# A hybrid attention decoder layer on one core: the out-projection weights' transfers moved from SyncE's queue to GpSimd's, their low parts to a buffer of their own

## Chip, cores, metric

The kernel runs on one core of one Trainium2 chip. The metric is the device time of one execution in microseconds (us); a kernel's time is the median of its runs. Engines are named as in the profile: PE (TensorE, matmuls), PEld (TensorE's weight loads), DVE (VectorE), ACT (ScalarE), POOL (GpSimd), SP (SyncE, which here only issues DMAs). Each engine works through its own queue in order; an instruction that waits holds up everything behind it on that engine.

## The reference, cut to what matters

One layer, sequence 1024, width 1024, float32:

```python
h = rms_norm(x, pre_g)
z = h @ w_in                       # 1024 x 7184: q, k, v, gate for 8 attention heads,
                                   # q, k, v, gate for 4 gated heads, 16 columns for the decay
oa = diff_attention(qa, ka, va, lam)   # softmax(q1 k1) - lam * softmax(q2 k2), causal
oa = rms_norm(oa, subln_g) * (1 - lam_init) * silu(ga)
ob = gla_chunked(qb, kb, vb, log_a)    # gated linear attention
ob = rms_norm(ob, gla_g) * silu(gb)
y = concat([oa, ob]) @ w_out       # 2048 x 1024
out = x + rms_norm(y, post_g)
```

Matmuls keep float32 accuracy by splitting each operand in a high part (rounded to TensorE's fp32r format) and a low part (the rest), and by summing three products: high by high, low by high, high by low.

## The kernel before, in words

**Stages.** First (to about 640 us) the in-projection; in its last two thirds the gated heads run between its steps. Then attention of the eight heads, with the out-projection of finished parts woven in, and a short end. Matmuls are issued through `mm` (line 117), which pins them: the order of PE's instructions is the program's. The other engines' orders are made by the framework's scheduler, which takes the instructions as their inputs and buffers come free in its own simulated time.

**The in-projection.** `pairs` lists 28 blocks of 256 columns of `w_in`. Each is computed by a Strassen-like scheme in seven products, numbered 1, 2, 5, 6, 4, 7, 3; `order` lists all (pair, product). A step (`step`, called by `go`) is one entry: 12 matmuls of 512 columns, or 24 of 256 columns in each of two pairs that run side by side ("wide" pairs, for values). `load_raw` (line 194) fetches a pair's raw weights from SP in two halves (`w_raw`, four buffers). `make_weights` subtracts blocks on DVE (line 296), rounds to the high part on ACT (315) and takes the low part on DVE (316), up to four steps ahead into a ring of five buffers. After product 1, 6 and 7 ACT copies a bank (`s`, 427); DVE adds (440); results go by way of the buffers `c` and `st`, four of each, to DRAM from SP (367, 377 and others).

**The out-projection's weights.** `w_out` (2048 x 1024) is split in high and low parts once, during the in-projection, and the parts go back to DRAM (`wod`), from where `weights` (909) loads them for the out-projection. `wo_step(n)`, called by `go` after each step of pairs 6 and up (n is the product's number), does this for one block of 128 x 512 floats (256 KB) at a time; there are 32 blocks:

- at n = 1 or 6 it takes the block that is open: ACT rounds it to `wo_hi` (584; a buffer of the ring `c`), DVE writes the low part over the raw block (586), and SP stores both (588);
- at n = 2 or 4 it opens the next one: SP loads 256 KB of `w_out` into `wo_raw` (592).

`wo_raw` has a single buffer. As the low part lies in it, the next load can't start before the low part's store has landed.

**The gated heads.** `gla`, a generator of which `go` runs one piece after each step from (12, 5) on, works through 4 heads in 2 halves each. `gla_loads` (745) fetches queries, keys, values (`kq`, `gv`) and the decayed queries `gqd` (754), the latter into a buffer with the tag `q1`, which has room for 1024 floats a partition and of which `gqd` takes 512. POOL's only work in this part is the causal select on the scores of a half, `gan` (775), which the matmuls `gpo` read some steps later. After the in-projection `load_qk` puts the first head's queries into `q1`.

Of the kernel before, what the change touches and what calls it, by code (L numbers as in the profile page):

```python
# [8 lines left out]
F32 = mybir.dt.float32  # L9
F32R = mybir.dt.float32r  # L10
# [4 lines left out]
P = 128  # L15
# [16 lines left out]
def hymba_kernel(  # L32
# [21 lines left out]
    act, dve, pool, pe, sp = nc.scalar, nc.vector, nc.gpsimd, nc.tensor, nc.sync  # L54

    def fp(t):
        return t.bitcast(F32)

    def cols(half):
        return slice(half * 512, half * 512 + 512)  # L60
# [38 lines left out]
    wod = [tc.dram_tile([2, P, D], F32, name=f"wo{e}_d") for e in range(2 * D // P)]  # L99
# [53 lines left out]
    kp = ctx.enter_context(tc.tile_pool(name="kp", bufs=1))  # L153
# [6 lines left out]
    def t_c(name, dt=F32):  # L160
        return t2k("c", 4, name, dt)
# [413 lines left out]


    wo_todo = [(e % 16, dh) for e in range(8, 24) for dh in range(2)]
    wo_open = []

    def wo_step(n):  # L580
        if n in (1, 6) and wo_open:
            e, dh, raw = wo_open.pop()
            hi = t_c("wo_hi", F32R)
            act.copy(hi, raw)
            lo = raw.bitcast(F32R)
            dve.tensor_tensor(lo, raw, fp(hi), ALU.subtract)
            for t, src in enumerate((hi, lo)):
                sp.dma_start(wod[e][t][:, cols(dh)], fp(src))
        if n in (2, 4) and wo_todo:
            e, dh = wo_todo.pop(0)  # L590
            raw = ap.tile([P, 512], F32, tag="t4", name="wo_raw", bufs=1)
            sp.dma_start(raw, w_out[0, e * P : (e + 1) * P, cols(dh)])
            wo_open.append((e, dh, raw))

    def go(n):
        for _ in range(n):
            i = made[0]
            if i == len(order):
                return
            made[0] = i + 1  # L600
            for a in range(4):
                prepare(i + a)
            step(i)
            if order[i][0] > EARLY and not (wide(order[i][0]) and order[i][0] % 2):
                wo_step(order[i][1])
            if fill and next(fill[0], 0) == 0:
                fill.pop(0)
# [135 lines left out]
    def gla_loads(g, half):  # L743

        if g < GLA_HEADS and (g, half) not in loaded:
            cs = cols(half)
            kq = kp.tile([P, 2, 512], F32, tag="q0", name="kq")
            v = kp.tile([P, 2, 4, P], F32, tag="k0", name="gv")
            qd = kp.tile([P, 512], F32, tag="q1", name="gqd")
            sp.dma_start(kq[:, 0], gq_d[g][2, :, cs])  # L750
            sp.dma_start(kq[:, 1], gq_d[g][0, :, cs])
            for t in range(2):
                sp.dma_start(v[:, t], gv_d[g][t, :, half * 4 : half * 4 + 4, :])
            sp.dma_start(qd, gq_d[g][1, :, cs])
            loaded[g, half] = kq, v, qd
        return loaded.get((g, half))

    def gla(g):

        u = None  # L760
        for half in range(2):
            cs = cols(half)
            kq, v, qd = gla_loads(g, half)
            gates = kp.tile([P, 2, 512], F32, tag="ks1", name="gg")
            yield
# [43 lines left out]
            for m in range(2):  # L809
# [13 lines left out]
                free.append(ib)  # L823
            yield
            gla_loads(*((g, 1) if half == 0 else (g + 1, 0)))

            sqs = kp.tile([P, 2, 512], F32, tag="k1", name="sqs")
# [697 lines left out]
```

## Time and profile before

| | us |
|---|---|
| median of 3 runs | 981.83 |
| all runs | 981.83, 982.66, 979.48 |
| the profiled execution | 982.58 |
| its span, first to last instruction | 980.8 |
| PE busy in the span | 957.4 (98%) |
| DVE busy | 735.6 (75%) |
| ACT busy | 600.6 (61%) |
| POOL busy | 138.9 (14%) |

The 1.8 us between the span and the profiled execution's time lie outside the first and last instruction. "Busy" for PE runs to modelled ends of pipelined matmuls. A wait in the lists below reads: engine, what it was about to do, line, then "<-" and what ended the wait; total us, times, longest.

### The profile page before, as it was taken

Reading aid. Unit: us, or ns where it says so; the run is one execution under the profiler, and the core shown is the slowest. Engines: PE = TensorE matmul, PEld = TensorE weight load, DVE = VectorE, ACT = ScalarE, POOL = GpSimd, SP = SyncE. Lnnn points to the kernel's source line nnn. Section 1 sums busy time; section 2 is a strip of 40 time slices with the busy share of each in tenths; the row PEclk is TensorE's granted clock in tenths of the full one; section 3 lists DMA queues with packets and bytes.
Section 4 is the critical chain, followed back from the end, with each engine's and each line's share of the span. In section 5 each row is a group of like instructions: output and inputs, shape, how many; then the busy total and the mean of one; then the engine's idle time right before and its main releaser. Section 6 shows DMA issues by size and latency. Waiting matters only on the chain.

```text
span 980.8 us, 15654 instructions
## 1 busy us (share of the span) xinstructions
PE 957.4 (98%) x5282; PEld 828.7 (84%) x5282; DVE 735.6 (75%) x1452; ACT 600.6 (61%) x1164; POOL 138.9 (14%) x158
## 2 busy tenths in 40 slices
PE   5999999999999999999999999999999999999997
PEld 5998988888889998899887888878888888888785
DVE  6887597798866677586785876487888888898554
ACT  8742455487357455445465775365777687887773
POOL 4300000000000010000000101121322222443322
PEclk9999999999999999999999999999999999999999
DMA  9442456656674868887887766997656769995777
GB/s 348 146 112 90 137 137 206 229 174 234 239 245 160 265 202 275 246 265 253 284 256 241 258 207 186 413 290 247 217 167 222 243 198 353 345 283 112 151 208 146
DMA packets 152593, 220.45 MB, mean 225 GB/s; under 512 B 17104, under 2 KB 83664, under 8 KB 152416
## 3 DMA queue, kind: packets, MB, share of 16 engines
q1 hardware_dynamic: 146176, 203.71, 64.2%
q0 software_dynamic: 6336, 15.73, 7.1%
q8 instruction: 42, 0.69, 0.3%
q14 instruction: 39, 0.32, 0.1%
HBM read 133.93 MB, written 88.60 MB: 227 GB/s over the span
## 4 chain that ended last, share of the span: by engine, by line
PE 83%; DVE 5%; DMA 5%; ACT 3%; issue 2%; SPq 1%; POOL 0%; DVEq 0%; ACTq 0%; POOLq 0%
PE x L117 20%; PE ypart L117 13%; PE y L117 13%; PE z L117 13%; PE sc L117 7%; PE po L117 5%; PE yps L117 4%; PE wtr L120 3%; PE gpo L117 1%; DMA w_raw<-in_w_in_dram 1%; DMA wo_raw<-in_w_out_dram 1%; DVE w L316 1%; DMA wo_d<-wo_raw 1%; PE gkl_ps L117 1%; DMA x<-in_x_dram 1%
## 5 line engine op out<-in xcount | busy, mean ns | idle before, releaser
L315 ACT CAST w<-w_raw 128x512 fp32r<-128x512 f32 (+1 forms) x164 | 112.2, 688 | 91.3 <-PE y L117 43.2
L316 DVE TENSOR_TENSOR w<-w_raw,w 128x512 fp32r<-128x512 f32 (+1 forms) x164 | 126.3, 773 | 51.6 <-ACT w L315 44.7
L1048 ACT ACTIVATE p<-p,stt 128x896 f32<-128x896 f32 (+7 forms) x128 | 99.3, 777 | 36.8 <-DVE stt L1038 34.0
L427 ACT COPY s<-x 128x512 f32<-128x512 f32 x84 | 49.1, 585 | 87.6 <-PE x L117 87.2
L296 DVE TENSOR_TENSOR w_raw<-w_raw 128x512 f32<-128x512 f32 (+1 forms) x96 | 75.8, 789 | 16.1 <-DMA w_raw<-in_w_in_dram 14.7
L1038 DVE CUSTOM_DVE_ANT_0 p<-sc,maskt 128x512 f32<-128x512 f32 (+3 forms) x128 | 74.2, 584 | 14.6 <-PE sc L117 13.5
L775 POOL TENSOR_SCALAR_AFFINE_SELECT gan<-gan 128x512 f32<-128x512 f32 x8 | 12.7, 1588 | 493.7 <-ACT gan L774 493.7
L117 PE MATMUL x<-s_hi,w 128*128 128x512 f32 x320 | 79.9, 392 | 1.9 <-ACT s L427 1.9
L117 PE MATMUL y<-h_hi,w 128*128 128x512 f32 x320 | 79.9, 392 | 0.0
L117 PE MATMUL ypart<-wo_hi,m_hi 128*128 128x512 f32 x192 | 79.5, 414 | 0.1
L117 PE MATMUL z<-s_hi,w 128*128 128x512 f32 x320 | 79.6, 391 | 0.0
L1054 POOL TENSOR_SCALAR p<-p,stt,lam 128x1024 f32<-128x1024 f32 (+3 forms) x64 | 56.1, 876 | 147.0 <-DVE stt L1053 144.6
L117 PE MATMUL ypart<-wo_hi,m_lo 128*128 128x512 f32 x192 | 75.5, 393 | 0.0
L117 PE MATMUL ypart<-wo_lo,m_hi 128*128 128x512 f32 x192 | 75.4, 393 | 0.0
L117 PEld LDWEIGHTS x<-s_hi,w 128*128 128x128 f32 x320 | 59.8, 188 | 14.5 <-ACT s L427 2.3
L117 PE MATMUL sc<-k,q 128*128 128x512 f32 (+1 forms) x192 | 69.1, 363 | 1.2 <-DVE stt L1038 1.2
L117 PEld LDWEIGHTS y<-h_hi,w 128*128 128x128 f32 x320 | 59.8, 188 | 12.3
L117 PEld LDWEIGHTS z<-s_hi,w 128*128 128x128 f32 x320 | 59.5, 188 | 12.0
L117 PE MATMUL sc<-ks,q 128*128 128x512 f32 (+1 forms) x192 | 66.1, 347 | 0.0
L1096 ACT CAST wt_hi<-wtr 128x512 fp32r<-128x512 f32 (+1 forms) x80 | 42.7, 534 | 24.8 <-PE wtr L120 24.0
L1097 DVE TENSOR_TENSOR wt_lo<-wtr,wt_hi 128x512 fp32r<-128x512 f32 (+1 forms) x80 | 50.6, 632 | 8.8 <-ACT wt_hi L1096 8.0
L1057 DVE SCALAR_TENSOR_TENSOR p<-p,stt,p 128x1024 f32<-128x1024 f32 (+3 forms) x64 | 52.1, 813 | 4.1 <-POOL p L1054 3.8
(226 smaller groups left out, 2245.0 us busy)
## 6 DMA issues: line engine op xcount, KB each, us to landing
w_raw<-in_w_in_dram SPq DMA_DIRECT2D x56, 512.0 KB, 4.6
wo_raw<-in_w_out_dram SPq DMA_DIRECT2D x32, 256.0 KB, 3.0
wo_d<-wo_hi SPq DMA_DIRECT2D x32, 256.0 KB, 2.7
wo_d<-wo_raw SPq DMA_DIRECT2D x32, 256.0 KB, 2.7
q<-q_d SPq DMA_DIRECT2D x32, 256.0 KB, 4.9
k<-k_d SPq DMA_DIRECT2D x32, 256.0 KB, 5.6
ks<-k_d SPq DMA_DIRECT2D x64, 128.0 KB, 5.8
v<-v_d SPq DMA_DIRECT2D x16, 512.0 KB, 7.6
```

Of the source, the lines that this page charges most:

```text
L117: tc.keep_in_program_order(pe.matmul(*a, **k))
L120: tc.keep_in_program_order(pe.transpose(dst, src, ident))
L296: dve.tensor_tensor(dst, a, b, ALU.subtract)
L315: act.copy(w[0], src)
L316: dve.tensor_tensor(w[1], src, fp(w[0]), ALU.subtract)
L427: act.copy(b[k], ps)
L1038: ins = dve.tensor_tensor_reduce(p[:, a:e], sc[:, : e - a], maskt[:, NZ + P - (e - a) :] if last else maskt[:, : e - a], 1.0, 3e38 if i == ...
L1048: act.activation(p[:, :n], p[:, :n], AF.Exp, bias=st[:, m : m + 1], scale=-1.0, accum_out=st[:, 2 + m : 3 + m],)
L1054: pool.tensor_scalar(p1[:, :n], p1[:, :n], st[:, 5:6], lam, ALU.mult, ALU.mult)
L1057: dve.scalar_tensor_tensor(p0[:, :n], p0[:, :n], st[:, 4:5], p1[:, :n], ALU.mult, ALU.subtract)
L1096: act.copy(hi[:, :n], pt[:, :n])
L1097: dve.tensor_tensor(lo[:, :n], pt[:, :n], fp(hi[:, :n]), ALU.subtract)
```

## The change

```diff
-    wo_open = []
+    wo_open, spare = [], []
 
     def wo_step(n):
         if n in (1, 6) and wo_open:
             e, dh, raw = wo_open.pop()
             hi = t_c("wo_hi", F32R)
             act.copy(hi, raw)
-            lo = raw.bitcast(F32R)
+            lo = (spare[0][:, 1] if spare else raw).bitcast(F32R)
             dve.tensor_tensor(lo, raw, fp(hi), ALU.subtract)
             for t, src in enumerate((hi, lo)):
-                sp.dma_start(wod[e][t][:, cols(dh)], fp(src))
-        if n in (2, 4) and wo_todo:
+                pool.dma_start(wod[e][t][:, cols(dh)], fp(src))
+        if n in ((1, 6) if spare else (2, 4)) and wo_todo and not wo_open:
             e, dh = wo_todo.pop(0)
             raw = ap.tile([P, 512], F32, tag="t4", name="wo_raw", bufs=1)
-            sp.dma_start(raw, w_out[0, e * P : (e + 1) * P, cols(dh)])
+            src = w_out[0, e * P : (e + 1) * P, cols(dh)]
+            if len(wo_todo) == 31:
+                sp.dma_start(raw, src)
+            else:
+                tc.keep_in_program_order(pool.dma_start(raw, src))
             wo_open.append((e, dh, raw))
...
-            qd = kp.tile([P, 512], F32, tag="q1", name="gqd")
+            if not spare:
+                spare.append(kp.tile([P, 2, 512], F32, tag="q1", name="gqd"))
+            qd = spare[0][:, 0]
```

All 64 stores of the parts and 31 of the 32 raw loads go from SP's queue to POOL's; the loads are pinned among POOL's pinned instructions. From the first `gla_loads` on, one buffer in `q1` serves all halves of the gated heads: `gqd` in its first 512 floats, the low part of the open block in its second. From then on a raw block is only read by the split, and the next load stands right behind the split, at n = 1 and 6. Up to then (blocks 1 to 12) the low part still lies over the raw block, and loads stay at n = 2 and 4.

## Prediction

> **What bounds the kernel now.** I read the page first: the busy times and the chain that ended last.
>
> ```profile
> PE 957.4 (98%) x5282; PEld 828.7 (84%) x5282; DVE 735.6 (75%) x1452; ACT 600.6 (61%) x1164; POOL 138.9 (14%) x158
> PE 83%; DVE 5%; DMA 5%; ACT 3%; issue 2%; SPq 1%; POOL 0%; DVEq 0%; ACTq 0%; POOLq 0%
> ```
>
> PE is busy 98% of the span, and its matmuls and their order stay as they are. The change can win only where PE stands idle because of the out-projection's weights. So the second view is busy time by windows, over the 400 us in which these blocks are made.
>
> ```profile
> 160.00:400.00 240.00, 240.00 (x1288) 208.29 (x1287) 179.64 (x278) 136.06 (x233) 6.84 (x4) 1.00 0.69 226
> 400.00:480.00 80.00, 79.26 (x551) 74.00 (x550) 58.12 (x86) 40.98 (x69) 1.51 (x2) 1.00 0.83 259
> 480.00:560.00 80.00, 77.93 (x389) 65.73 (x388) 56.72 (x94) 47.63 (x88) 4.35 (x2) 1.00 0.81 256
> ```
>
> The columns are the window, its length, then busy us of PE, PEld, DVE, ACT and POOL, PE's clock, the DMA engines' share, GB/s. PE loses nothing up to 400 us, 0.74 in the next 80 and 2.07 in the last: 2.81 us in all. That is the size of the prize, 0.3% of the time, which is also about what a measurement of this kernel can tell from no change.
>
> Third view, the waits: for the block's load on ACT, and on SP for the store that frees the buffer.
>
> ```profile
> ACT wo_hi L584 <- DMA wo_raw<-in_w_out_dram: 33.4, 14, 10.4
> ```
>
> ```profile
> SPq L592 <- DMA wo_d<-wo_raw: 49.9, 26, 4.8
> ```
>
> ACT stands 33.4 us in front of raw blocks that have not landed, once for 10.4. SP's queue stands 49.9 us, up to 4.8 at a time, until a low part's store lands, with everything else that SP issues behind it.
>
> **The longest stall, step by step,** in the timeline (start, duration, what; in brackets the idle time before it): first ACT alone, then the block's steps on DVE and SP, then PE alone.
>
> ```profile
> 524.89 0.62 ACT L584 CAST wo_hi<-wo_raw 128x512 fp32r<-128x512 f32 x1 [10.44 <-DMA wo_raw<-in_w_out_dram]
> 525.42 0.58 ACT L427 COPY s<-x 128x512 f32<-128x512 f32 x1
> ```
>
> ```profile
> 506.19 0.68 DVE L586 TENSOR_TENSOR wo_raw<-wo_raw,wo_hi 128x512 fp32r<-128x512 f32 x1
> ...
> 515.83 0.59 SPq L588 DMA_DIRECT2D wo_d<-wo_raw  x1
> ...
> 518.38 0.33 SPq L592 DMA_DIRECT2D wo_raw<-in_w_out_dram  x1
> ```
>
> ```profile
> 520.82 0.83 PE L117 MATMUL gpo<-gan,gv 128*128 128x128 f32 x6
> ...
> 523.71 0.39 PE L117 MATMUL gpo<-gqd,gu 128*128 128x128 f32 x2
> 526.05 1.20 PE L117 MATMUL x<-s_hi,w 128*128 128x512 f32 x4 [1.95 <-ACT s L427]
> ```
>
> The low part was ready at 506.9, but its store stood in SP's queue until 515.83; the next load came out at 518.38, and ACT, in order, waited for it with the copy `s` behind, which PE needed. The six gpo matmuls take 0.11 each from start to start, so after the two at 523.71 PE was due at 523.93; it came at 526.05: 2.12 us lost. An ACT wait of 10.44 costs 2.12, so some 8.3 us of it were free.
>
> The second stall is at 410, with PE's rows by themselves behind:
>
> ```profile
> 398.36 0.57 SPq L592 DMA_DIRECT2D wo_raw<-in_w_out_dram  x1
> ...
> 402.55 0.43 SPq L194 DMA_DIRECT2D w_raw<-in_w_in_dram  x1
> ...
> 409.05 1.22 DVE L296 TENSOR_TENSOR w_raw<-w_raw 128x1024 f32<-128x1024 f32 x1 [3.39 <-DMA w_raw<-in_w_in_dram]
> ```
>
> ```profile
> 409.59 0.39 PE L117 MATMUL gpo<-gan,gv 128*128 128x128 f32 x2
> 410.72 0.49 PE L117 MATMUL gpo<-gqd,gu 128*128 128x128 f32 x2 [0.74 <-DVE gu L802]
> ```
>
> SP issues one transfer every half microsecond or so here, the block's among them, and comes late to the load of `w_raw`. DVE waits 3.39 for it, in order, with the state `gu` behind, and PE, due at 409.81, comes at 410.72: 0.91 lost. A third, small one at 498, ACT's row and then PE's:
>
> ```profile
> 495.05 0.62 ACT L584 CAST wo_hi<-wo_raw 128x512 fp32r<-128x512 f32 x1 [3.60 <-DMA wo_raw<-in_w_out_dram]
> ```
>
> ```profile
> 496.83 1.07 PE L117 MATMUL y<-h_lo,w 128*128 128x512 f32 x4
> 497.74 1.02 PE L117 MATMUL gms<-sq_hl,ones 128*128 128x512 f32 x2
> 498.60 0.64 PE L117 MATMUL x<-s_hi,w 128*128 128x512 f32 x2
> ```
>
> ACT is held 3.60, and the split of the gated norm's squares, behind it, comes late. Four y matmuls take 0.91 from start to start; the two gms take 0.86 instead of 0.45: 0.41 lost. The three lose 2.12 + 0.91 + 0.41 = 3.4 us, of which 2.81 shows as idle time.
>
> **The change, part by part.**
>
> *Transfers off SP.* 64 stores and 31 loads leave SP's queue, with the 49.9 us of waits. At 402 the load of the block (0.57) no longer stands ahead of `w_raw`, nor what SP was behind by from earlier ones; about 1 us sooner, enough for the 0.91. SP is on the chain for 1% only, so its issue time is worth nothing elsewhere.
>
> *The raw buffer freed by the split (blocks 13 to 32).* The load no longer waits for a landing; it goes out behind the two stores. What transfers cost POOL, and how long they take to land (KB each, us):
>
> ```profile
> L909 POOL DMA_DIRECT2D wo_hi<-wo_d x8: 527/527/775, 606.0 to 626.4; - x8
> ```
>
> ```profile
> wo_raw<-in_w_out_dram SPq DMA_DIRECT2D x32, 256.0 KB, 3.0
> wo_d<-wo_raw SPq DMA_DIRECT2D x32, 256.0 KB, 2.7
> ...
> wo_hi<-wo_d POOLq DMA_DIRECT2D x8, 512.0 KB, 9.9
> y_d<-yst POOLq DMA_DIRECT2D x16, 256.0 KB, 5.0
> ```
>
> Three issues of 0.53 and a landing of 3.0 (as from SP) to 9.9 (twice the size, sixteen issued in a row): the raw block lies ready 4.6 to 11.5 us after the split. I take 6.6, by POOL's 256 KB row. The closest splits of before are 7.4 apart (ACT at 524.89, above, and here):
>
> ```profile
> 532.25 0.62 ACT L584 CAST wo_hi<-wo_raw 128x512 fp32r<-128x512 f32 x1 [2.00 <-DMA wo_raw<-in_w_out_dram]
> ```
>
> So ACT no longer waits for a block, and the stalls at 498 and 524 go. At 11.5 it would wait 4.1, less than the 8.3 that were free. What is late next at 524: PE was done with x when it went on to gpo at 520.82 at the latest, so ACT can copy it 3 us ahead of PE's need.
>
> *A new wait.* From block 13 on DVE, before it writes the low part into the single new place, waits until the last low part's store is done. Behind it stand DVE's weight parts (L316), and PE behind these. Of 7.4 us between splits, DVE takes 0.7 and POOL's two issues 1.1: a landing up to 5.6 is free. Before, a store and a load had to land in that time, one after the other; now the store alone. Cost taken: 0, by the row of 5.0; at 9.9, 4.3 us of DVE's time at the closest pair, again under 8.3. *The ring `c`* waits for the high part's store as before, which now leaves when the split is done and not when SP comes to it: 0, and below zero is possible.
>
> *POOL's queue.* 95 issues at 0.53 are 50 us, where POOL is nearly idle (12.7 us busy in the 400). Behind them stands the causal select, eight times:
>
> ```profile
> 508.93 0.85 POOL L775 TENSOR_SCALAR_AFFINE_SELECT gan<-gan 128x512 f32<-128x512 f32 x1 [35.92 <-ACT gan L774]
> ```
>
> It ended at 509.8 and gpo, which reads it, began at 520.82: 11 us of slack. POOL can be held by a split that is due (a few us) and three issues (1.6). Cost 0, or what lies over 11 if that cover is gone.
>
> *Blocks 1 to 12, still in place.* Here a store's landing, an issue and a load's landing stand in a row, as on SP, but each may be longer: an issue by 0.2, a landing by nothing (SP's rows) to 2.3 us (5.0 for 2.7). Up to 280 us ACT's waits for raw blocks are small, and splits come every 9.5 us on average:
>
> ```profile
> ACT wo_hi L584 <- DMA wo_raw<-in_w_out_dram: 3.7, 5, 1.6
> ```
>
> ```profile
> L586 DVE TENSOR_TENSOR wo_raw<-wo_raw,wo_hi x12: 682/684/693, 171.9 to 276.1; 128x512 fp32r<-128x512 f32 x12
> ```
>
> Each may grow by 0.4 to 5 us. The wait of 3.60 at 495 cost PE 0.41, and 8.3 of the longest were free. I take 0.4 us for the twelve together, between 0 and 5 (12 times 0.41).
>
> *Sum.* −3.4 + 0.4 = −3.0: from the profiled execution's 982.58 to 979.6. That execution lies 0.75 over the median of the runs shown, so from 981.83 to **978.8**.
>
> **Rivals.**
>
> *Only issue time is saved.* If ACT still finds raw blocks late, because the data's way and not SP's queue holds them (the DMA engines are 0.8 busy from 400 to 560), only the backlog at 402 goes: 981.83 − 0.9 = 980.9. Against it: at 515.83 the store had stood ready for 9 us, in a queue. The Trainium skill ("DMA: Bandwidth & Descriptors", section "Issuing engines are not separate DMA queues") says that several issuing engines save only the sequencer's time to start a transfer, usually small beside the transfer. By that rule this rival would hold; the trace speaks against it, since SP loses waits in an in-order queue and not only issues.
>
> *Slower: POOL's transfers land too late in blocks 1 to 12.* Place: ACT at L584 from 160 to 280 us. After a split come two issues (1.1), a landing, an issue (0.5), a landing, in 9.5 us; with 8.3 free, ACT's wait begins to cost when each landing takes over (9.5 + 8.3 − 1.6) / 2 = 8.1 us. From there every microsecond more costs two in each of twelve blocks. At 8.5 that is 0.8 × 12 = 9.6, less the 3.4 won: 988. The 512 KB row (9.9) speaks for it, the 256 KB row (5.0) against. The Trainium skill ("SBUF — State Buffer", section "SBUF: two separate sides") warns that GpSimd can't write its descriptors while VectorE runs certain copies in a two-port mode; issues of 527 ns, 775 at the most, show no such delay here.
>
> *The orders of ACT, DVE and SP move.* The scheduler places them by its own times. It could put a late load or copy ahead of something that PE needs, here or in attention. Two new stalls of the largest size seen (2.1) would take the gain and 1.2 us more: 983.
>
> **How the numbers follow.** The forecast has 0.55, within 977.6 to 979.6; in seven tenths of it the time is below 978.88 (0.3% less). Only issue time: 0.17. Slower by late landings: 0.16. Orders moved: 0.12, mostly to the slow side. So faster by over 0.3%: 0.40; within: 0.36; slower: 0.24. The range goes from 977.4 to 985.0: it holds the forecast, the second case, the moved orders and the beginning of the slow case; most of the latter is left out.
>
> **What would show it.** Right: no ACT wait on `wo_raw` from 280 us on, 80.00 or nearly for PE in the windows from 400 to 560, SP's waits at L588 and L592 gone, raw loads out within 2 us of the split. Wrong: POOL's 256 KB transfers landing in over 8 us; a wait of DVE at L586 for a DMA; gpo waiting for POOL; PE idle in a window that has none now.

## The result, and the profile after

| | before | after |
|---|---|---|
| median of 19 runs each, us | 980.54 | 978.44 |
| lowest to highest | 978.16 to 983.67 | 977.09 to 979.63 |
| the profiled execution | 982.58 | 978.49 |
| its span | 980.8 | 976.7 |

The ratio is 0.9975, with a 95% interval of 0.9965 to 0.9984: 2.5 us less, a quarter of a per cent (the medians lie 2.1 apart, the means 2.6). That is under the 0.3% which the prediction took as what a measurement of this kernel can tell from no change, but the interval leaves no change out: it is a gain, and a small one. The spread of the runs fell from 5.5 to 2.5 us. The profiled execution of before stood 2.0 us over the median of its 19 runs, so the two profiles lie further apart (4.1 us of span) than the kernels do.

Busy time by windows in the kernel after, the columns as in the prediction:

```profile
160.00:400.00 240.00, 239.77 (x1286) 207.81 (x1285) 179.61 (x278) 137.21 (x235) 39.80 (x66) 1.00 0.70 230
400.00:480.00 80.00, 80.00 (x556) 74.84 (x555) 56.70 (x84) 39.00 (x66) 12.41 (x14) 1.00 0.82 261
480.00:560.00 80.00, 80.00 (x414) 68.42 (x413) 61.26 (x100) 55.11 (x100) 14.27 (x22) 1.00 0.82 259
```

PE's second number is its busy time: nothing is lost from 400 to 560, where 2.81 us were; 0.23 is lost before 400, where nothing was. POOL (the fifth pair) has 66 us of work where it had 13, and no engine waits for POOL itself in this stretch. The chain that ended last now holds PE for 93% instead of 83%, DMA for 1% instead of 5%:

```profile
PE 93%; DVE 3%; ACT 2%; DMA 1%; issue 1%; POOL 0%; DVEq 0%; SPq 0%; ACTq 0%; POOLq 0%
```

The place of the longest stall, after, on POOL and then on ACT and PE:

```profile
513.93 0.56 POOL L588 DMA_DIRECT2D wo_d<-wo_hi  x1 [6.24 <-ACT wo_hi L584]
514.91 0.54 POOL L588 DMA_DIRECT2D wo_d<-gqd  x1 [0.43 <-DVE gqd L586]
515.72 0.55 POOL L596 DMA_DIRECT2D wo_raw<-in_w_out_dram  x1 [0.27 <-issue]
```

```profile
525.08 0.59 ACT L427 COPY s<-x 128x512 f32<-128x512 f32 x1 [0.91 <-PE x L117]
525.56 0.62 ACT L315 CAST w<-w_raw 128x512 fp32r<-128x512 f32 x1
526.08 0.62 ACT L584 CAST wo_hi<-wo_raw 128x512 fp32r<-128x512 f32 x1
```

```profile
521.92 0.39 PE L117 MATMUL gpo<-gqd,gu 128*128 128x128 f32 x2
522.06 2.07 PE L117 MATMUL x<-s_hi,w 128*128 128x512 f32 x8
```

The low part (now a part of the tile `gqd`) and the next raw load leave within 3 us of the split at 513, and ACT comes to that block at 526 with no bracket: it waited for nothing. PE goes from gpo to x without a gap. ACT's waits for raw blocks, and the largest sum of waits in SP's queue, in the kernel after:

```profile
ACT wo_hi L584 <- DMA wo_raw<-in_w_out_dram: 11.3, 7, 3.4
```

```profile
SPq L194 <- DVE w L316: 81.2, 30, 11.0
```

33.4 us became 11.3, the longest 10.4 became 3.4. The waits of SP's queue at L588 and L592 are gone. SP didn't gain idle time of use: it now comes early to the loads of `w_raw` and waits there for their buffers, 81.2 us where it was 39.5.

One stall is new, at 363:

```profile
362.89 0.69 DVE L411 TENSOR_TENSOR c<-y,s 128x512 f32<-128x512 f32 x1 [3.07 <-DMA v_d<-c]
```

```profile
362.37 1.03 PE L117 MATMUL kv<-gv,gan 128*128 128x256 f32 x4
363.63 1.13 PE L117 MATMUL kv<-gv,gan 128*128 128x256 f32 x4 [0.23 <-DVE c L411]
```

DVE waits 3.07 for a store of values to free a buffer of the ring `c`, and PE, behind, loses 0.23 idle.

ACT's longest wait for a raw block, 3.43, has a new cause. POOL's rows, then ACT's:

```profile
465.70 0.54 POOL L588 DMA_DIRECT2D wo_d<-wo_hi  x1 [7.38 <-ACT wo_hi L584]
467.72 5.30 POOL L781 TENSOR_SCALAR_AFFINE_SELECT gan<-gan 128x512 f32<-128x512 f32 x1 [1.48 <-ACT gan L780]
472.98 0.56 POOL L588 DMA_DIRECT2D wo_d<-gqd  x1
473.53 0.55 POOL L596 DMA_DIRECT2D wo_raw<-in_w_out_dram  x1
```

```profile
464.78 0.62 ACT L584 CAST wo_hi<-wo_raw 128x512 fp32r<-128x512 f32 x1 [0.56 <-ACT w L315]
479.89 0.62 ACT L584 CAST wo_hi<-wo_raw 128x512 fp32r<-128x512 f32 x1 [3.43 <-DMA wo_raw<-in_w_out_dram]
```

The causal select stood ahead of the low part's store and the load, which left 8.8 us after the split instead of about 3 (so it did in the second profile). By the profile the select ran for 5.30 us, where the eight have a median of 1.3; why is not known. PE lost nothing by it.

### The profile page after: what moved, and what is told of

It is laid out like the page before. It is cut to its first block, busy times and chain, and to the rows that moved or that the text cites. A ratio compares the mean times of both kernels' runs of the same rounds, so it can differ in the third digit from the quotient of the medians.

```text
span 976.7 us, 15689 instructions
## 1 busy us (share of the span) xinstructions
PE 956.6 (98%) x5282; PEld 828.3 (85%) x5282; DVE 735.4 (75%) x1452; ACT 602.1 (62%) x1164; POOL 193.8 (20%) x253
## 4 chain that ended last, share of the span: by engine, by line
PE 93%; DVE 3%; ACT 2%; DMA 1%; issue 1%; POOL 0%; DVEq 0%; SPq 0%; ACTq 0%; POOLq 0%
PE x L117 23%; PE y L117 15%; PE z L117 15%; PE ypart L117 13%; PE sc L117 7%; PE po L117 5%; PE yps L117 4%; PE wtr L120 3%; PE gpo L117 3%; PE kv L117 1%; PE gkl_ps L117 1%; PE pa L117 1%; DMA v_d<-c 1%; PE xT L120 0%; ACT junk L491 0%
## 5 line engine op out<-in xcount | busy, mean ns | idle before, releaser
L316 DVE TENSOR_TENSOR w<-w_raw,w 128x512 fp32r<-128x512 f32 (+1 forms) x164 | 126.6, 773 | 57.0 <-ACT w L315 48.8
L588 POOL DMA_DIRECT2D wo_d<-wo_hi x32 | 17.6, 550 | 349.7 <-ACT wo_hi L584 349.7
```

The costliest lines, as they stand in the source:

```text
L316: dve.tensor_tensor(w[1], src, fp(w[0]), ALU.subtract)
```

## The experiments

The kernels of one timed group shared a chip and the runs of before. PE idle is counted from 160 to 560 us in one profile; ACT's wait is that for raw blocks (`ACT wo_hi L584 <- DMA wo_raw<-in_w_out_dram`).

| kernel | ratio to before (95%) | PE idle, us | ACT's wait, total, longest |
|---|---|---|---|
| before, three profiles | 1 | 2.81, 3.15, 2.49 | 33.4, 38.1, 36.8; 10.4, 9.4, 9.9 |
| the change, two profiles | 0.9975 (0.9965 to 0.9984) | 0.23, 0.36 | 11.3, 11.0; 3.4, 3.3 |
| POOL's queue alone, three profiles | 1.0002 (0.9990 to 1.0014) | 1.21, 0.32, 0.74 | 26.0, 24.9, 24.5; 5.2, 5.2, 4.2 |
| freed buffer alone, on SP | 0.9981 (0.9970 to 0.9993) | 0.67 | 9.1; 3.1 |
| two of 32 blocks | 0.9979 (0.9969 to 0.9989) | 0.00 | none |
| stores on POOL, loads on SP | 0.9977 (0.9967 to 0.9988) | 0.56 | 13.9; 3.3 |
| two raw buffers, on SP | 0.9980 (0.9970 to 0.9989) | 0.00 | 5.4; 1.7 |
| one more landing | 1.0133 (1.0116 to 1.0149) | 10.94 | 31.5; 5.4 |
| two more landings | 1.0504 (1.0486 to 1.0522) | 37.08 | 60.0; 9.4 |

**POOL's queue alone.** The change without its buffer (`gqd` has a buffer to itself again, as in the kernel before):

```diff
-            lo = (spare[0][:, 1] if spare else raw).bitcast(F32R)
+            lo = raw.bitcast(F32R)
-        if n in ((1, 6) if spare else (2, 4)) and wo_todo and not wo_open:
+        if n in (2, 4) and wo_todo:
```

> All transfers of the blocks from POOL as in the change, but the low part still over the raw block and the loads at n = 2 and 4, for all 32 blocks. Queue theory (SP's in-order queue made the blocks late): the stores and loads leave on time, the stalls at 410, 498 and 524 go, ratio to before 0.997 to 0.998. Buffer theory (the landing that the load must wait for made them late): ACT still waits for raw blocks by 8 us and more at places and PE keeps a stall of about 2 us, ratio 0.999 to 1.000. Order theory (the scheduler's new orders made the gain): a ratio unlike the change's, with PE stalls at new places.

Timed, it gains nothing: 1.0002. Its profile shows what the queue can't help, the wait for the landing of the store that lies in the way of the next load:

```profile
POOL wo_raw L596 <- DMA wo_d<-wo_raw: 101.3, 29, 6.4
```

What stood on SP (49.9 us) now stands on POOL, and ACT still waits 26.0 us for raw blocks. The buffer theory's price (a stall of 2 us, behind ACT waits of over 8) is not in this profile, though; ACT's longest is 5.2. I took two more profiles:

> The kernel with POOL's queue alone (low part over the raw block) for a second profile. Its median was that of before, so by the sampled-stall theory PE's idle time between 160 and 560 us should again be of 1 to 4 us, at other places than in its first profile (364 and 409), with ACT waiting for raw blocks by over 5 us ahead of the larger ones.

> POOL's queue alone, a third profile. Its median over 12 runs (980.78) was that of before, yet its first two profiles show 1.2 and 0.3 us of idle PE between 160 and 560 us where before shows 2.5 to 3.2. If these two were lucky, the third shows 2 to 4 us there, with an ACT wait of over 8 us ahead of the largest; if the kernel loses in another place, PE idles there (0 to 160 or 560 to 980 us) by 1.5 us more than in before.

Both expectations missed on PE's idle time: all three profiles show 0.3 to 1.2 us of idle PE where before has 2.5 to 3.2, and no other place where the kernel loses as much more (0.57 at 567 in the second). The stall at 524 is in none of them. At 410 the load of `w_raw` goes out at 400.58, 398.05 and 397.38 (in the three profiles of before at 402.55, 402.09 and 402.09), and only the first profile has a stall there. It is not the old one; SP's row, DVE's and PE's:

```profile
400.58 0.59 SPq L194 DMA_DIRECT2D w_raw<-in_w_in_dram  x1
```

```profile
406.73 1.23 DVE L296 TENSOR_TENSOR w_raw<-w_raw 128x1024 f32<-128x1024 f32 x1 [4.17 <-DMA w_raw<-in_w_in_dram]
407.87 1.22 DVE L316 TENSOR_TENSOR w<-w_raw,w 128x1024 fp32r<-128x1024 f32 x1
409.00 1.58 DVE L806 SCALAR_TENSOR_TENSOR gu<-gu,dstep,kv 128x256 f32<-128x256 f32 x3
```

```profile
409.53 0.49 PE L117 MATMUL gpo<-gqd,gu 128*128 128x128 f32 x2 [0.56 <-DVE gu L806]
```

`w_raw` has landed 2.3 us sooner than in before (406.73, not 409.05), but in this kernel's order DVE makes a weight part (L316) between it and `gu`.

Against these profiles stands the timing: a median of 980.78 over 12 runs, beside 980.46. The three profiled executions took 980.37, 979.19 and 978.56, all below that median, while single runs went up to 983.42; where the slower ones lose their time no profile shows. So the timing says that the queue alone brings nothing, the profiles of its faster executions say that it takes the stalls away, and this stays open.

**The freed buffer alone**, every transfer on SP: `pool.dma_start` is `sp.dma_start` again in the change's two places, and the loads are not pinned.

> The low part in its own place and the loads at n = 1 and 6 as in the change, but every transfer from SP. Queue theory: the block's store and load still stand in SP's backlog, w_raw's load too; the load leaves about 2 us sooner than before at the worst place, so most of the 2.1 goes there and the 0.9 at 410 stays: ratio 0.998 to 0.9995. Buffer theory: ACT hardly waits for blocks, ratio 0.997 to 0.998, as the whole change. Order theory: a ratio unlike both.

0.9981 and ACT waits of 9.1 us. The ratio itself lies in the queue theory's range, just outside the buffer theory's, and its interval covers both; what decides are the stalls. Those at 498 and 524 are gone, and the one at 410 too, which the queue theory wanted to stay: `w_raw`'s load goes out at 401.51, 0.6 to 1.0 us sooner than in before, with the block's issues still ahead of it in SP's queue. In the same group of runs this kernel has a median of 978.72 and no run above 979.84, POOL's queue alone one of 980.78 and runs up to 983.42. What PE loses here, 0.67, is at 363.

**Two of 32 blocks.** `wo_todo` has two entries, and `weights` loads all from `wod[8]`.

> The kernel before with 2 of the 32 blocks made (the weights for the out-projection are all loaded from these, so the output is not the reference's). It tells what the blocks can cost at all. If they cost PE only the three stalls, 3.4 us of the 980.5, the ratio is 0.9965 and the change (0.9975) leaves at most 1 us. If ACT's and DVE's time for the splits costs PE too, the ratio is 0.994 or less.

0.9979, above both: three stalls of 3.4 us are too much (0.9965 lies outside the interval), and ACT's and DVE's time for the splits costs PE nothing that can be seen. By the ratio, leaving out nearly all the work on the blocks brings no more than the change; by the medians it is 2.6 us against 2.1, a difference inside the intervals. PE's idle time allows the change at most its own 0.2 to 0.4 us more.

**Stores on POOL, loads on SP.** The change with `sp.dma_start(raw, src)` for every load.

> The change with the raw loads from SP and the stores from POOL. Queue theory: the loads stand in SP's queue and wait there for the split, and hold what is behind them; but the block is loaded a step pair ahead, so ACT seldom waits: ratio 0.9975 to 0.999. Buffer theory: as the whole change, 0.997 to 0.998.

0.9977. With the buffer freed it makes no difference that can be seen which queue issues what.

**Is one profile a fair sample?** Both kernels again, unchanged.

> The kernel before, unchanged, for a second profile. If the stalls at 410, 498 and 524 belong to the program, they stand there again with about the same sizes. If they hang on how fast the DMAs of that execution were, they are elsewhere or of other sizes, and PE's idle time between 160 and 560 us lies anywhere between 0 and 5 us, going up and down with the execution's time (978 to 984.6).

> The kernel before, unchanged, for a third profile; as for the second.

> The changed kernel, unchanged, for a second profile. PE idle between 160 and 560 us at most 1 us, the only stall at 363 (values' store v_d), if at all; ACT's waits for raw blocks below 4 us each.

PE's waits from 160 to 560 us in the second profile of before (in total, times, longest):

```profile
PE gpo L117 <- DVE gu L802: 1.7, 1, 1.7
PE x L117 <- ACT s L427: 0.9, 1, 0.9
PE gms L117 <- DVE sq_hl L834: 0.6, 1, 0.6
```

and in the third:

```profile
PE x L117 <- ACT s L427: 1.7, 1, 1.7
PE gpo L117 <- DVE gu L802: 0.8, 1, 0.8
```

gpo's row is the stall at 409, x's the one at 523, and that of gms the one at 498. The stalls at 409 and 523 are in all three profiles of before, so they belong to the program; their sizes move (idle 0.74, 1.66, 0.81 and 1.95, 0.90, 1.68), and the third, at 498, is missing in one. The mean idle time of before is 2.8 us, of after 0.3. The difference, 2.5 us, is the gain by the ratio; as all three profiled executions of before (982.58, 981.83, 980.59) were slower than its median, some of this agreement is chance.

**Two raw buffers.** The kernel before, with loads at n = 2 and 4 and all on SP, but every other block from 13 on goes to the free half of `q1`:

```diff
-            raw = ap.tile([P, 512], F32, tag="t4", name="wo_raw", bufs=1)
+            if spare and len(wo_todo) % 2:
+                raw = spare[0][:, 1]
+            else:
+                raw = ap.tile([P, 512], F32, tag="t4", name="wo_raw", bufs=1)
```

> The kernel before (SP issues all, loads at n = 2 and 4, low part over the raw block), with a second raw buffer in the free half of the queries' buffer, taken in turn from block 13 on. A load then waits for the store of two blocks ago. If what counts is only that a load need not wait for the last store's landing, ACT's waits for raw blocks fall from 33 to 38 us to under 15, the stalls at 409 and 524 go, and the ratio is 0.9970 to 0.9985. If the earlier place of the load (n = 1 and 6) is needed too, a stall of 1 us or more stays and the ratio is 0.9985 to 1.000.

0.9980, no idle PE at all in the stretch, ACT's waits 5.4 us:

```profile
160.00:400.00 240.00, 240.00 (x1289) 208.34 (x1288) 180.04 (x280) 137.23 (x235) 7.05 (x4) 1.00 0.71 228
400.00:480.00 80.00, 80.00 (x556) 74.83 (x555) 58.31 (x88) 40.53 (x70) 5.98 (x2) 1.00 0.84 263
480.00:560.00 80.00, 80.00 (x413) 68.47 (x412) 59.43 (x97) 53.21 (x96) 4.07 (x2) 1.00 0.84 263
```

Neither POOL's queue nor the earlier place of the load is needed. What counts is that a load need not wait for the landing of the store just before it. The stall at 363 isn't here.

**More landings.** To see how much lateness is free, the low part's store of blocks 1 to 12 was made two and three times, each waiting for the one before:

```diff
-                pool.dma_start(wod[e][t][:, cols(dh)], fp(src))
+                for _ in range(2 if t and not spare else 1):
+                    pool.dma_start(wod[e][t][:, cols(dh)], fp(src))
```

> The change, with the low part's store of blocks 1 to 12 made twice, one after the other, so that their raw loads leave about 3 us later (0.5 issue, 2.2 landing, 0.3). Split to split the chain is then some 11.5 us, where steps give 9.5. Prediction's rule (8.3 us of each ACT wait are free): ACT waits 2 to 4 us in each block and PE loses nothing, ratio to before 0.9970 to 0.998. Rival (the chain runs from split to split, so what it is too long adds up and is free only once): 12 times 2 less 8.3, about 16 us lost, ratio about 1.014, with PE idle between 200 and 300 us.

> As the last, with the store made three times: the loads leave about 6 us later, the chain is some 14.5 us. Prediction's rule: ACT waits 5 to 8 us in each block, still free, ratio 0.997 to 0.999. Rival (adds up): 12 times 5 less 8.3, about 50 us lost, ratio about 1.05, PE idle all along from 180 to 340 us.

1.0133 and 1.0504, where lateness that adds up gave 1.014 and 1.05, and the prediction's rule at most 0.999. One turn of the chain with one more landing, POOL's rows and ACT's:

```profile
271.28 0.54 POOL L589 DMA_DIRECT2D wo_d<-wo_hi  x1 [4.44 <-ACT wo_hi L584]
272.01 0.54 POOL L589 DMA_DIRECT2D wo_d<-wo_raw  x1 [0.19 <-issue]
274.93 0.54 POOL L589 DMA_DIRECT2D wo_d<-wo_raw  x1 [2.38 <-DMA wo_d<-wo_raw]
278.75 0.55 POOL L597 DMA_DIRECT2D wo_raw<-in_w_out_dram  x1 [3.27 <-DMA wo_d<-wo_raw]
```

```profile
270.37 0.62 ACT L584 CAST wo_hi<-wo_raw 128x512 fp32r<-128x512 f32 x1 [5.38 <-DMA wo_raw<-in_w_out_dram]
...
282.39 0.62 ACT L584 CAST wo_hi<-wo_raw 128x512 fp32r<-128x512 f32 x1 [5.44 <-issue]
```

From split to split it is 12.0 us: split, store, landing, store, landing, load, landing, split (for the second wait the profile names no releaser). ACT's first and thirteenth split, in the kernel after, with one more landing and with two:

```profile
157.73 0.62 ACT L584 CAST wo_hi<-wo_raw 128x512 fp32r<-128x512 f32 x1
276.08 0.62 ACT L584 CAST wo_hi<-wo_raw 128x512 fp32r<-128x512 f32 x1 [0.39 <-DMA wo_raw<-in_w_out_dram]
```

```profile
157.52 0.61 ACT L584 CAST wo_hi<-wo_raw 128x512 fp32r<-128x512 f32 x1
306.81 0.62 ACT L584 CAST wo_hi<-wo_raw 128x512 fp32r<-128x512 f32 x1 [5.47 <-issue]
```

```profile
157.63 0.61 ACT L584 CAST wo_hi<-wo_raw 128x512 fp32r<-128x512 f32 x1
343.06 0.61 ACT L584 CAST wo_hi<-wo_raw 128x512 fp32r<-128x512 f32 x1
```

The twelve turns take 118, 149 and 185 us, 9.9, 12.4 and 15.5 each: the thirteenth split is 31 and 67 us late against the kernel after. The spans (991.4 and 1029.1, beside 976.7) are 14.7 and 52.4 longer. So of the lateness of all twelve blocks together some 15 us were free, once. That is the rival's form; its sizes were off, in ways that cancel: the turns are longer than the 11.5 and 14.5 assumed, and more than 8.3 us are free. PE does not pay at every block: with one more landing it stands five times between 204 and 302 us, longest 3.78.

## Why the prediction was right, and where it was not

*What bounds it, and the size of the prize.* Right. PE's idle time from 160 to 560 us was all that could be won: without nearly all the work on the blocks the ratio is 0.9979. That 978.44 lies only 0.4 from the 978.8 forecast is luck in part: the forecast was counted from 981.83, the median of three runs, which is 1.3 above the median of 19, and its gain of 3.0 is 0.9 above the 2.1 between the medians; the two errors nearly cancel.

*The three stalls, 3.4 us.* This term was mis-sized. The stalls are real, but the sum took the start-to-start loss, 0.6 us more than shows as idle time. Idle time is what the change won: 2.81 in that profile, 2.8 on average over three, of which 0.3 is left after. The third stall is not in every execution. The gain was 2.5 by the ratio, not 3.0 (0.9975, not 0.9969).

*"Transfers off SP ... enough for the 0.91".* The path was right, but it isn't the only one. Against the three profiles of before `w_raw`'s load left 8 us sooner in the kernel after (394.00) and 1.5 to 5.2 sooner with POOL's queue alone, and the old stall at 410 is in none of these. With the buffer freed and every transfer on SP it left 0.6 to 1.0 sooner, and in its one profile the stall is gone too. What the step had wrong is that the transfers must leave SP: with the freed buffer they need not, and without it their leaving brought no gain that the timing shows. The same holds for the longest stall, where I read nine microseconds in SP's queue as the cause.

*The raw buffer freed.* Right, and by the timing the whole of it. Not as quick as said: the raw load goes out 3.1 us after the split's start (median of blocks 13 to 31; 2.2 to 8.8), as the split itself and DVE's low part come before it, and lands in 4.9 (median), near the 5.0 taken. So the block lies ready after about 8 us, not 6.6. Two of the signs named for a right prediction therefore failed without a cost: loads out within 2 us of the split, and no ACT wait from 280 us on (there is one, 3.43).

*The new wait of DVE.* It did not come: DVE at L586 waits for ACT alone (3.9 us on the new place), never for the store. POOL's issues took 0.54, not 0.53. PE never waited for the causal select, as said; that the select can hold the block's load was not foreseen (464 to 480, above).

*Blocks 1 to 12, 0.4 us.* PE lost nothing there. But the rule behind this step, and behind the slower rival, was wrong: it gave every wait 8.3 free microseconds. The chain goes from split to split, so lateness is handed on and the slack is there once, some 15 us. In the changed kernel as it stands the chain of these blocks is about as long as the steps (ACT waits for five of them, up to 2.7 us): one landing more costs 15 us of span against it, 13 against the kernel before.

*The 0.23 at 363* was not foreseen. It is one of the prediction's signs of being wrong, "PE idle in a window that has none now". In the kernel after, a store of values took 5.5 us from 357.3 on, in before 3.9 from 358.6; DVE then waits 2.9 to 3.5 for it in the change, with POOL's queue alone, with the freed buffer on SP and with the stores on POOL, and 2.0 to 2.3 in before, with two blocks and with two raw buffers. Why was not settled.

*Only issue time is saved* (980.9): refuted for the change, as 978.44 is below it by more than its interval. For the queue alone it fits the timing (1.0002), and the argument set against it, that SP lost waits and not only issues, did not carry: the waits went along to POOL. *The orders move* (983): no sign of it; every stretch from 560 us on has the same idle PE within 0.1 us.

## What to carry to other kernels

A single buffer that is loaded, worked on in place, stored and loaded again makes a loop of two landings. Add up the loop from one use to the next and compare it with the time that the bounding engine gives it: if the two are close, a slow transfer or a late queue is handed on from turn to turn and shows up as a stall far away once the slack is used up. Here a second place for either half ended it, whichever queue issued the transfers. When a profile shows a transfer late in a queue, ask what the queue was waiting for before you move the transfer. And size a gain of a few microseconds by the idle time in several profiles, and count the forecast from a median of many runs.

## What the hardware showed besides

The clock granted to PE can fall when PE stands idle. With two more landings, the window with the most idle time (columns as above; in the windows of the kernel after the clock is 1.00):

```profile
240.00:320.00 80.00, 54.85 (x210) 43.24 (x208) 40.74 (x65) 26.22 (x49) 14.09 (x26) 0.85 0.56 193
```

PE is busy 54.85 of 80 us at a clock of 0.85, so a long stall can cost more than its length: in that kernel eight kv matmuls at 336 took 2.89 us from start to start after a stall of 2.88; in the kernel before, without one, they took 1.53 at 513. Over the whole kernel PE's 5282 matmuls are busy 972.1 us, 15.5 more than in the kernel after, and idle 36.9 more: together the 52.4 of span. The Trainium skill ("TensorE: Matmul & The Clock Gate", section "Part 1: The HAM clock gate (the "warmup" mystery)") says that TensorE drops to half its clock after an idle window of about 3.4 us. The trace agrees in kind, but shows it after shorter stalls: the 2.88 above, and, with one more landing, 2.08 at 226, after which eight x matmuls took 3.21 us (clock 0.63 from 226 to 230), where they took 1.96 after a stall of 0.82 at 204. The length alone doesn't decide: after 2.23 at 302 eight kv matmuls took 1.61. Stalls of 0.2 to 2 us in before and after leave the clock at 1.00 in their windows.
